# Memory keys as a fused layer's first products, its input loaded feature-major, and a gate's last chunks behind the attention heads

## The chip, the cores and the metric

One core of one Trainium2 chip runs the whole program. The metric is device time in microseconds (us) of one execution, the median of several. Beside it there is a profile of one execution by the hardware profiler.

The engines go by short names here: PE (TensorE) multiplies matrices; PEld is its load of weights; DVE (VectorE) and ACT (ScalarE) do elementwise work; POOL (GpSimd) does small work and starts accumulating DMAs; SP (SyncE) starts the loads. Each engine executes its own list of instructions strictly in the order in which the program wrote them, and waits on semaphores for the others.

## The reference

256 positions, width 1024, one layer, float32.

```python
n = rmsnorm(x) * g_mix
z = n @ w_in            # c_a, c_g, q, k, v, qi, ki, wi, gc, ga by columns
u = c_a * sigmoid(c_g)                      # the conv's input
u = causal_conv(u, 31 taps, per channel) + conv_b
y_conv = silu(layernorm(u)) @ w_conv_out
y_attn = attention(q, k, v, keys chosen by qi, ki, wi; 8 heads of 128) @ w_attn_out
h = x + (sigmoid(gc + b) * y_conv + sigmoid(ga + b) * y_attn) @ w_mix_out
m = rmsnorm(mem) * g_mem                    # 256 memory tokens
k2, v2 = split(m @ wx_kv)                   # 4 heads of 128
h = h + cross_attention(rmsnorm(h) * g_x @ wx_q, k2, v2) @ wx_o
h = h + relu(rmsnorm(h) * g_ffn @ w_ff1)**2 @ w_ff2
out = rmsnorm(h) * g_final
```

## The kernel before

**Products.** A float32 value is split into a high part of a shorter format (fp32r) and the low rest; a product is hi·hi + hi·lo + lo·hi. An activation's pair lies in a `Parts` tile (`n_p` for the normed input, `mem_p` for the memory, `o_p` for the heads' outputs, `u_p` for the normed conv), 8 blocks of 128 features (k, or kt) in two tiles of four. A tile of output is 128 features by 256 positions, and takes 8 k. In a *wide* tile the weights' high part is multiplied with both parts of the activation at once (512 columns), and the weights' low part with the high part (256 columns): two instructions for each k. The two 256-column halves of the bank are then added: ACT copies one half, DVE adds the other (`merge`).

**Weights.** `STREAM` lists the chunks of 1 MB (256 features each, two output tiles) in the order in which SP's queue loads them (`load`) and in which they are used. Names: conv (c_a and c_g), qi, ki, gc, ga, v, q, k, the memory's keys xk and values xv, ao (w_attn_out), co (w_conv_out), mix, and so on. A half chunk is split by ACT (`hi<-raw`) and DVE (`lo<-raw,hi`), a few halves ahead of its products. A chunk in `WHOLE` is not split: its products are made natively in float32, against an activation that is not split either. In the kernel before only the first conv chunk is such, against `n_f`.

**What sets the order.** Everything is written in the order in which the engines run it. Products of a stage are emitted tile by tile; between tiles `tick()` advances the chains in progress (generators: `head` for each attention head, `gate` for a gate, `memory` for the memory's norm, `layer_norm` for the conv) by one step, and then fills DVE's list with conv taps (`fill_one`) as long as the counted time of DVE is less than that of PE. So an edit of the chunk order moves steps of unlike chains against each other. Some taps go another way: ACT makes products and a POOL DMA accumulates them (`add_some`).

**The start.** `x` is loaded position-major (`x_rm`, two 512 KB loads), PE transposes it by 16 products (`pt_n`) after five warm-up products, ACT and DVE sum the squares of its rows (`ss_n`), POOL makes the reciprocal root (`rs_n`), PE spreads it over the partitions (`ps_rsb_n`), ACT and DVE apply the gain (`xg`), DVE multiplies (`n_f`) and the first conv products follow. The memory is read later in two layouts, `mem_rm` for the row norms and `mem_t` for the products, and nine steps of `memory` make its pair `mem_p`.

**The heads and behind them.** Each head is a chain: scores `ps_s`, masked maximum on DVE (`att_t`, `mx`), Exp on ACT (`att_p<-att_t,mx`), reciprocal on DVE, scale on ACT (`att_p<-att_p,sm`), transposes on PE (`ps_pt`), the product `ps_o`, the pair `o_p`. The last heads are covered by the products of xk and xv. Then ao (its merge gives `ya`, which is multiplied into the gate's tile `ga_t`) and co. Once all eight conv tiles have their 31 taps (`done`), `layer_norm` starts: PE averages over the features (`ps_mub`), DVE subtracts the mean (`acc<-acc,ps_mub`), ACT squares, DVE sums (`vs`), POOL makes the root, PE spreads it (`ps_rsb`), DVE multiplies, ACT applies Silu, and ACT and DVE write the pair `u_p`, two k at a time, which the co products read. An Exp, a Sigmoid and a Silu need different tables in ACT; changing them is an `ACT_TABLE_LOAD`.

Of the kernel before, what the change touches and what calls it, by code (L numbers as in the profile page):

```python
# [111 lines left out]
def block_kernel(ctx, tc, x, xt, mem, memt, wst, wki, vecs, convw, gout, out):  # L112
# [256 lines left out]
    nc.vector.tensor_copy(zero_r, zero)
# [10 lines left out]
    nc.scalar.activation(half, half, AF.Sigmoid, bias=0.0, scale=0.0)  # L380
    nc.gpsimd.memset(half, -0.5)
    ps = ps_aux("ps_warm")
    for j in range(5):
        nc.tensor.matmul(ps, zero_r[:, :P], zero_r, start=True, stop=True)
# [30 lines left out]
    ss = small.tile([P, 2], F32, tag="ss", name="ss_n")
    ptn = [ps_acc(f"pt_n{c}") for c in range(4)]
    xg = t8("xg")
    ss2 = small.tile([P, 2], F32, tag="ss2", name="ss2_n")
    nc.gpsimd.memset(ss2, EPS)
    junk = w2("junk_full", BF16, (P, D))  # L420
    act(junk, x_rm[:, 0, :], AF.Square, scale=1.0 / 32, accum_out=ss[:, 0:1])
# [4 lines left out]
    junk = w2("junk_half", BF16, (P, D))  # L426
    act(junk[:, : D // 2], x_rm[:, 1, : D // 2], AF.Square, scale=1.0 / 32, accum_out=ss[:, 1:2])
    dve.tensor_tensor_reduce(out=n_f[:, 0:2, :].rearrange("p k s -> p (k s)"), in0=x_rm[:, 1, D // 2 :],
                             in1=x_rm[:, 1, D // 2 :], scale=1.0 / D, scalar=EPS, op0=ALU.mult, op1=ALU.add,
                             accum_out=ss2[:, 1:2])  # L430
    dve.tensor_tensor(out=ss, in0=ss, in1=ss2, op=ALU.add)
    rs_n = power(ss, "n")
    rsb_n = spread(rs_n, "rsb_n")
    for kt in range(KT):
        src = ptn[kt // 2][:, (kt % 2) * S : (kt % 2) * S + S]
        if kt in (4, 6):
            dve.tensor_scalar(xg[:, kt, :], src, g_first[:, kt : kt + 1], None, ALU.mult)
        else:
            act(xg[:, kt, :], src, AF.Copy, scale=g_first[:, kt : kt + 1])
    for lo, hi in ((0, 1), (1, 2), (2, 4), (4, 6), (6, 8)):  # L440
        dve.tensor_tensor(out=n_f[:, lo:hi, :], in0=xg[:, lo:hi, :],
                          in1=rsb_n.unsqueeze(1).to_broadcast([P, hi - lo, S]), op=ALU.mult)
# [12 lines left out]
    def memory():
        mem_rm = t8("mem_rm", F32, (P, 2, D))
        mem_t = t8("mem_t")
# [12 lines left out]
        act(mrb, spread(rs_m, "mrb"), AF.Copy)  # L470
        for kt in range(KT + 1):
            if kt < KT:
                act(mem2.high(kt), mem_t[:, kt, :], AF.Copy, scale=g_mem[:, kt : kt + 1])
            if kt > 0:
                j = kt - 1
                dve.scalar_tensor_tensor(out=mem2.low(j), in0=mem_t[:, j, :], scalar=g_mem[:, j : j + 1],
                                         in1=mem2.high(j).bitcast(F32), op0=ALU.mult, op1=ALU.subtract)
            yield
# [51 lines left out]
    def conv_in(i):  # L530
# [106 lines left out]
        act(t, src, AF.Sigmoid, bias=b)
# [127 lines left out]
    kv = t8("kv", F32, (P, 2, XH * S))
    kx = kv[:, 0, :].rearrange("p (h n) -> p h n", h=XH)
    vx = kv[:, 1, :].rearrange("p (r n) -> p r n", r=2)
    for i in range(2):
        form_b("xk", i, mem2, copy_to(kx), ps_turn)
# [487 lines left out]
```

## Time and profile before

| | |
|---|---|
| time, median of 3 runs | 508.91 us (508.64 to 509.0) |
| the profiled execution's own time | 508.65 us |
| its span | 506.8 us |
| first conv product on PE | 8.74 us after the span's start |
| DMA read / written | 91.16 MB / 1.05 MB |

The span is the time from the first to the last recorded instruction; what the profiled execution took beyond it lies around it. In a chain row the first two numbers are start and length of a piece in us; in a timeline row start and summed length of a group of like instructions, with what ended the idle time ahead of it in square brackets. A group row has the count behind an x, then busy us and the mean of one in ns. Nearly all instructions of PE and DVE carry the line of the helper that records them (L77 before, L78 after), so they are told apart by their tiles.

### The profile page before, as it was taken

Reading aid. Unit: us, or ns where it says so; the run is one execution under the profiler, and the core shown is the slowest. Engines: PE = TensorE matmul, PEld = TensorE weight load, DVE = VectorE, ACT = ScalarE, POOL = GpSimd, SP = SyncE. Lnnn points to the kernel's source line nnn. Section 1 sums busy time; section 2 is a strip of 40 time slices with the busy share of each in tenths; the row PEclk is TensorE's granted clock in tenths of the full one; section 3 lists DMA queues with packets and bytes.
Section 4 is the critical chain, followed back from the end, with each engine's and each line's share of the span. In section 5 each row is a group of like instructions: output and inputs, shape, how many; then the busy total and the mean of one; then the engine's idle time right before and its main releaser. Section 6 shows DMA issues by size and latency. Waiting matters only on the chain.

```text
span 506.8 us, 7855 instructions
## 1 busy us (share of the span) xinstructions
PE 496.5 (98%) x2951; PEld 438.6 (87%) x2951; DVE 419.7 (83%) x806; ACT 314.6 (62%) x565; POOL 31.7 (6%) x49
## 2 busy tenths in 40 slices
PE   7999999999999999999999999999999999999994
PEld 5999998888888888888898999988888888888884
DVE  5999999999999799999899986699755666665565
ACT  7657777878666667678657666575444545544442
POOL 2002212221111100000000000000000000000000
PEclk9999999999999999999999999999999999999998
DMA  8959768899788634437644553445777744455302
GB/s 320 375 185 276 208 182 248 222 262 248 223 279 221 188 113 168 133 116 250 249 164 169 192 214 105 149 157 224 212 242 212 247 167 166 174 211 211 153 1 83
DMA packets 26502, 100.32 MB, mean 198 GB/s; under 512 B 10576, under 2 KB 11472, under 8 KB 15968
## 3 DMA queue, kind: packets, MB, share of 16 engines
q1 hardware_dynamic: 22400, 92.90, 52.5%
q0 software_dynamic: 3632, 6.59, 7.4%
q8 instruction: 23, 0.38, 0.3%
q10 hardware_dynamic: 432, 0.33, 0.2%
q14 instruction: 15, 0.12, 0.1%
HBM read 91.16 MB, written 1.05 MB: 182 GB/s over the span
## 4 chain that ended last, share of the span: by engine, by line
PE 95%; issue 1%; ACT 1%; DMA 1%; DVE 1%; POOLq 0%; POOL 0%; SPq 0%; DVEq 0%; ACTq 0%
PE ps_f L77 18%; PE ps_ff L77 16%; PE ps_conv L77 9%; PE ps_co L77 4%; PE ps_mix L77 4%; PE ps_ao L77 4%; PE ps_q L77 4%; PE ps_k L77 4%; PE ps_ga L77 4%; PE ps_gc L77 4%; PE ps_v L77 4%; PE ps_xo L77 3%; PE ps_qi L77 2%; PE ps_xk L77 2%; PE ps_xv L77 2%; PE ps_xq L77 2%
## 5 line engine op out<-in xcount | busy, mean ns | idle before, releaser
L77 DVE TENSOR_TENSOR lo<-raw,hi 128x1024 fp32r<-128x1024 f32 x163 | 196.8, 1216 | 5.0 <-ACT hi L189 3.4
L189 ACT ACTIVATE hi<-raw 128x1024 fp32r<-128x1024 f32 x163 | 168.8, 1048 | 1.6 <-DMA raw<-in_wst_dram 1.6
L77 PE MATMUL ps_f<-ff_p,hi 128*128 128x512 f32 x256 | 89.5, 396 | 0.0
L77 PE MATMUL ps_ff<-hi,fs 128*128 128x512 f32 (+1 forms) x256 | 80.4, 386 | 0.0
L77 DVE SCALAR_TENSOR_TENSOR acc<-u,cw,acc 128x234 f32<-128x234 f32 (+29 forms) x190 | 78.1, 462 | 0.3
L77 PE MATMUL ps_f<-ff_p,lo 128*128 128x256 f32 x256 | 66.1, 279 | 0.0
L77 PEld LDWEIGHTS ps_ff<-hi,fs 128*128 128x128 f32 x256 | 47.9, 188 | 9.2
L1084 ACT ACTIVATE ft<-ps_f 128x256 f32<-128x256 f32 x32 | 12.3, 383 | 70.0 <-PE ps_f L77 70.0
L77 PEld LDWEIGHTS ps_f<-ff_p,hi 128*128 128x128 f32 x256 | 46.7, 188 | 9.2
L77 DVE TENSOR_TENSOR ft<-ps_f,ft 128x256 f32<-128x256 f32 x32 | 13.5, 422 | 46.0 <-ACT ft L1084 46.0
L77 PEld LDWEIGHTS ps_f<-ff_p,lo 128*128 128x128 f32 x256 | 48.2, 188 | 2.7
L77 PE MATMUL ps_ff<-lo,fs 128*128 128x512 f32 (+1 forms) x128 | 49.4, 386 | 0.0
L77 PE MATMUL ps_conv<-n_p,hi 128*128 128x256 f32 x224 | 41.0, 285 | 0.0
L77 PEld LDWEIGHTS ps_conv<-n_p,hi 128*128 128x128 f32 x224 | 34.9, 192 | 0.8 <-issue 0.7
L77 PE MATMUL ps_conv<-n_p,lo 128*128 128x256 f32 x112 | 31.7, 283 | 0.0
L516 POOL DMA_DIRECT2D acc<-products x25 | 21.6, 866 | 125.3 <-ACT products L515 48.7
L77 PEld LDWEIGHTS ps_ff<-lo,fs 128*128 128x128 f32 x128 | 24.1, 188 | 4.9
L77 PE MATMUL ps_q<-n_p,hi 128*128 128x512 f32 x64 | 23.6, 406 | 0.0
L77 PE MATMUL ps_k<-n_p,hi 128*128 128x512 f32 x64 | 23.5, 407 | 0.0
L77 PE MATMUL ps_ao<-o_p,hi 128*128 128x512 f32 x64 | 22.6, 401 | 0.0
L77 PE MATMUL ps_co<-u_p,hi 128*128 128x512 f32 (+1 forms) x80 | 22.2, 351 | 0.0
L77 PE MATMUL ps_mix<-mix_p,hi 128*128 128x512 f32 (+1 forms) x80 | 22.2, 351 | 0.0
(246 smaller groups left out, 1009.4 us busy)
## 6 DMA issues: line engine op xcount, KB each, us to landing
raw<-in_wst_dram SPq DMA_DIRECT2D x80, 1024.0 KB, 4.9
acc<-products POOLq DMA_DIRECT2D x25, 256.0 KB, 5.0
raw<-in_wst_dram SPq DMA_DIRECT2D x4, 512.0 KB, 7.2
x_rm<-in_x_dram SPq DMA_DIRECT2D x2, 512.0 KB, 4.1
mem_rm<-in_mem_dram SPq DMA_DIRECT2D x1, 1024.0 KB, 8.7
mem_t<-in_memt_dram SPq DMA_DIRECT2D x1, 1024.0 KB, 10.7
h_t<-in_xt_dram SPq DMA_DIRECT2D x1, 1024.0 KB, 7.1
h_rm<-turned SPq DMA_DIRECT2D x16, 64.0 KB, 5.9
```

What stands on the lines that cost most here:

```text
L77: return fn(*args, **kwargs)
L189: act(hi, raw[:, ns], AF.Copy)
L516: nc.gpsimd.dma_start(acc[:, ts, :], prod, accum_op=ALU.add)
L1084: act(t, ps[:, S:], AF.Copy)
```

## The change

Two moves, and what goes with them.

*Memory keys first.* The two xk chunks are the stream's first. xk0 is multiplied natively (`native`) against `mem_g`, the gain times `mem_t`, and xk1 as two wide tiles against `mem_p`. `mem_t` and the first chunks are loaded in pieces that alternate on SP's queue. `x` comes feature-major as `x_t` from an input that the kernel already had, behind the first half of xk1, so the 16 transposes and the row sums go; ACT squares it, DVE adds over the k (`sums_n`), four small products (`ps_sq_n`) inside xk1's first tile sum over the partitions, and the root is spread inside xk1's second tile. `n_f` is made by four DVE steps with gain and root in one, and by four ACT scales with two DVE products. The warm-up is nine bf16 products instead of five. `vec` (the biases and gains) moves from POOL's queue to SP's, ahead of `cw`, and both behind the first conv chunks. The nine `mem_p` steps and the later `mem_t` load leave `memory`.

*The gate's last chunks.* Only ga 0 and 1 stand ahead of v; ga 2 and 3 stand behind q and k, where xk was. Their Sigmoid waits until all eight heads have had their Exp (`gate_late`), so that ACT's table changes once, and once more than before in all. `nused[0] < 5` becomes `< 7`, the number of half chunks used by then.

```diff
 STREAM = (
-    [("conv", i) for i in range(4)]
+    [("xk", i) for i in range(2)]
+    + [("conv", i) for i in range(4)]
...
-    + [("ga", i) for i in range(4)]
+    + [("ga", i) for i in range(2)]
     + [("v", i) for i in range(4)]
     + [(n, i) for i in range(4) for n in ("q", "k")]
-    + [("xk", i) for i in range(2)]
+    + [("ga", i) for i in range(2, 4)]
...
-WHOLE = (("conv", 0),)
+WHOLE = (("xk", 0), ("conv", 0))
...
-    x_rm = t8("x_rm", F32, (P, 2, D))
-    for rb in range(2):
-        nc.sync.dma_start(x_rm[:, rb, :], x[rb * P : (rb + 1) * P, :])
+    mem_t = t8("mem_t")
+    x_t = t8("x_t")
...
-    nc.gpsimd.dma_start(vec, vecs)
...
-    for parts in (2, 2, 1):
-        load(parts)
+    fetch(mem_t, memt, 0, 2)()
+    load((512, 1024), (fetch(mem_t, memt, 2, 5), fetch(mem_t, memt, 5, 8)))
+    load((1024,), (lambda: [fetch(x_t, xt, c, c + 4)() for c in (0, 4)],))
+    load((1024,))
+    load()
+    nc.sync.dma_start(vec, vecs)
     nc.sync.dma_start(cw, convw.rearrange("p (k t) -> p k t", k=KT))
-    load()
...
-    for j in range(5):
-        nc.tensor.matmul(ps, zero_r[:, :P], zero_r, start=True, stop=True)
+    for j in range(9):
+        nc.tensor.matmul(ps, zero[:, :P], zero, start=True, stop=True)
...
+    for kt in range(KT):
+        g = g_first[:, 1, kt : kt + 1]
+        if kt in (0, 2, 5):
+            act(mem_g[:, kt, :], mem_t[:, kt, :], AF.Copy, scale=g)
+        else:
+            dve.tensor_scalar(mem_g[:, kt, :], mem_t[:, kt, :], g, None, ALU.mult)
+    low_jobs_m = [mem_parts(kt) for kt in range(0, KT, 2)]
+    for job in low_jobs_m:
+        job()
+    ps_k0 = native(("xk", 0), 0, mem_g)
+    split_high()
+    split_low()
+    act(kx[:, 0, :], ps_k0, AF.Copy)
+    ps_k1 = native(("xk", 0), 1, mem_g)
+    adds = [x_square(kt) for kt in range(0, KT, 2)]
+    act(kx[:, 1, :], ps_k1, AF.Copy)
+    for add in adds:
+        add()
+    split_high()
+    load()
+    ws, banks = [], []
+    ws.append(weights("xk", 1, 0, KT))
+    banks.append(ps_acc("ps_xk10"))
+    tile_b(banks[0], ws[0], mem2, range(6), True)
+    ps = ps_aux("ps_sq_n")
     for rb in range(2):
-        for kt in range(KT):
-            pe.transpose(ptn[kt // 2][:, (kt % 2) * S + rb * P : (kt % 2) * S + rb * P + P],
-                         x_rm[:, rb, kt * P : kt * P + P], ident)
...
+        for j in range(2):
+            pe.matmul(ps[:, 2 * rb : 2 * rb + 2], sums_n[:, j, rb * P : rb * P + P], onesd[:, :2], start=j == 0,
+                      stop=j == 1)
+    ms = small.tile([P, 2], F32, tag="ms", name="ms_n")
+    dve.tensor_scalar(ms, ps[:, :4].rearrange("p (r t) -> p r t", r=2)[:, :, 0], EPS, None, ALU.add)
+    rs_n = power(ms, "n")
+    split_low()
+    tile_b(banks[0], ws[0], mem2, range(6, KT), True)
+    ws.append(weights("xk", 1, 1, KT))
+    banks.append(ps_acc("ps_xk11"))
+    ps = banks[1]
+    for lo, hi in ((0, 3), (3, 6)):
+        for kt in range(lo, hi):
+            pe.matmul(ps, ws[1][0][:, kt, :], mem2.both(kt), start=kt == 0, stop=False)
+        for kt in range(lo, hi):
+            pe.matmul(ps[:, S:], ws[1][1][:, kt, :], mem2.high(kt), start=False, stop=False)
+        if lo == 0:
+            rsb_n = spread(rs_n, "rsb_n")
+    tile_b(ps, ws[1], mem2, range(6, KT), True)
+    for kt in range(4, KT):
+        act(n_f[:, kt, :], x_t[:, kt, :], AF.Copy, scale=g_first[:, 0, kt : kt + 1])
+    for kt in range(4):
+        dve.scalar_tensor_tensor(out=n_f[:, kt, :], in0=x_t[:, kt, :], scalar=g_first[:, 0, kt : kt + 1], in1=rsb_n,
+                                 op0=ALU.mult, op1=ALU.mult)
+    for kt in (4, 6):
+        dve.tensor_tensor(out=n_f[:, kt : kt + 2, :], in0=n_f[:, kt : kt + 2, :],
+                          in1=rsb_n.unsqueeze(1).to_broadcast([P, 2, S]), op=ALU.mult)
...
     def memory():
...
-        nc.sync.dma_start(mem_t, memt)
...
-        for kt in range(KT + 1):
-            if kt < KT:
-                act(mem2.high(kt), mem_t[:, kt, :], AF.Copy, scale=g_mem[:, kt : kt + 1])
...
@@ in head
+        exped.append(h)
...
+    def gate_late(ct, ps):
+        yield from merge(ga_t[:, ct, :], ps)
+        while len(exped) < NH:
+            yield
+        act(ga_t[:, ct, :], ga_t[:, ct, :], AF.Sigmoid, bias=bga[:, ct : ct + 1])
+
+    late = []
+    for i in range(2, 4):
+        form_b("ga", i, n2, lambda ct, ps: late.append(start(gate_late(ct, ps))), ps_turn)
...
-    for c in heads:
+    for c in heads + late:
         finish(c)
```

Three places show how the lists of instructions differ. The first is PE at the start. The numbers behind the names only keep tiles apart. Before:

```order
L384 MATMUL ps_warm<-zero_r 128x512 x5
L77 MATMUL pt_n_128<-ident,x_rm 128x128 x2
...
L77 MATMUL pt_n_131<-ident,x_rm 128x128 x2
L77 MATMUL ps_rsb_n<-ident,rs_n 128x128 x2
L77 MATMUL ps_conv_203<-n_f,raw_89 128x256 x8
L77 MATMUL ps_conv_218<-n_f,raw_89 128x256 x8
L77 MATMUL ps_conv_237<-n_p_124,hi_0_183 128x256 x2
```

After (`ps_xk_156` and `_170` are the native tiles of xk0, `_195` and `_224` those of xk1, `ps_conv_282` the first conv tile):

```order
L390 MATMUL ps_warm<-zero 128x512
L78 MATMUL ps_xk_156<-mem_g,raw_88 128x256 x8
L78 MATMUL ps_xk_170<-mem_g,raw_88 128x256 x8
L78 MATMUL ps_xk_195<-mem_p_133,hi_0_165 128x512
...
L78 MATMUL ps_xk_195<-mem_p_134,hi_0_165 128x512
L78 MATMUL ps_sq_n<-onesd,sums_n 128x2 x4
L78 MATMUL ps_xk_195<-mem_p_134,lo_0_166 128x256
...
L78 MATMUL ps_xk_224<-mem_p_133,hi_1_190 128x512 x3
L78 MATMUL ps_xk_224<-mem_p_133,lo_1_191 128x256 x3
L78 MATMUL ps_rsb_n<-ident,rs_n 128x128 x2
L78 MATMUL ps_xk_224<-mem_p_133,hi_1_190 128x512
...
L78 MATMUL ps_conv_282<-n_f,raw_99 128x256 x8
```

The four xk tiles, with the sums of x and the spread inside them, now stand ahead of the first conv products, and the 16 transposes are gone.

The second is ACT at the last heads, from the last head's Exp (the rows with `sm` on the left) to the scale of the head before it. Before:

```order
L273 ACTIVATE o_p_1715<-ps_o_2459 128x256
L728 ACTIVATE att_p_2466,sm_2428<-att_t_2382,mx_2427 128x128
L728 ACTIVATE att_p_2466,sm_2428<-att_t_2382,mx_2427 128x256
L333 ACTIVATE kv<-ps_xk_2442 128x256
L189 ACTIVATE hi_0_2479<-raw_2309 128x1024
L734 ACTIVATE att_p_2424<-att_p_2424,sm_2375 128x128
L734 ACTIVATE att_p_2424<-att_p_2424,sm_2375 128x256
L189 ACTIVATE hi_1_2502<-raw_2309 128x1024
```

After:

```order
L276 ACTIVATE o_p_1669<-ps_o_2417 128x256
L778 ACTIVATE att_p_2424,sm_2386<-att_t_2340,mx_2385 128x128
L778 ACTIVATE att_p_2424,sm_2386<-att_t_2340,mx_2385 128x256
L820 ACT_TABLE_LOAD
L820 ACTIVATE ga_t<-ga_t,vec 128x256 x3
L336 ACTIVATE ga_t<-ps_ga_2400 128x256
L192 ACTIVATE hi_0_2442<-raw_2268 128x1024
L785 ACTIVATE att_p_2382<-att_p_2382,sm_2333 128x128
L785 ACTIVATE att_p_2382<-att_p_2382,sm_2333 128x256
L820 ACTIVATE ga_t<-ga_t,vec 128x256
```

A table load and three sigmoids now stand between the last Exp and the copy of the last tile's merge, the next split and the scale of head 6; a fourth sigmoid follows.

The third is PE behind the last head (`ps_o` is its product, `ps_ao` the first tile of ao). Before:

```order
L77 MATMUL ps_xv_2475<-hi_1_2439,mem_p_191 128x512
L77 MATMUL ps_o_2584<-ptr_2560,v_rm 128x128 x3
L77 MATMUL ps_mub<-usum,onesd 128x256
L77 MATMUL ps_ao_2614<-o_p_1714,hi_0_2479 128x512
L77 MATMUL ps_ao_2614<-o_p_1714,lo_0_2480 128x256 x2
L77 MATMUL ps_ao_2614<-o_p_1714,hi_0_2479 128x512
```

After:

```order
L78 MATMUL ps_o_2549<-ptr_2522,v_rm 128x128 x3
L78 MATMUL ps_ao_2563<-o_p_1668,hi_0_2442 128x512
L78 MATMUL ps_ao_2563<-o_p_1668,lo_0_2443 128x256 x2
...
L78 MATMUL ps_ao_2563<-o_p_1669,lo_0_2443 128x256
L78 MATMUL ps_ao_2563<-o_p_1669,hi_0_2442 128x512
L78 MATMUL ps_mub<-usum,onesd 128x256
L78 MATMUL ps_ao_2604<-o_p_1668,hi_1_2465 128x512
```

The product of the conv's mean stood ahead of the first ao tile and now stands behind it.

On DVE, from the pair of the last head (`o_p<-ps_o`) to the sums of squares, before:

```order
L77 TENSOR_TENSOR lo_0_2536<-raw_2390,hi_0_2535 128x1024
L77 TENSOR_TENSOR o_p_1715<-ps_o_2584,o_p_1715 128x256
L77 TENSOR_TENSOR acc<-acc,ps_mub 128x512 x3
L77 TENSOR_TENSOR vs<-vs,sq_vr_2598 128x512
L77 TENSOR_TENSOR acc<-acc,ps_mub 128x512
```

After:

```order
L78 TENSOR_TENSOR lo_0_2498<-raw_2348,hi_0_2497 128x1024
L78 TENSOR_TENSOR o_p_1669<-ps_o_2549,o_p_1669 128x256
L78 SCALAR_TENSOR_TENSOR acc<-u,cw,acc 128x226
L78 TENSOR_TENSOR usum<-usum,acc 128x256
L78 TENSOR_TENSOR lo_1_2533<-raw_2348,hi_1_2532 128x1024
L78 TENSOR_TENSOR acc<-acc,ps_mub 128x512 x3
L78 TENSOR_TENSOR vs<-vs,sq_vr_2588 128x512
L78 TENSOR_TENSOR acc<-acc,ps_mub 128x512
```

One conv tap, its sum and a split now stand between the pair of the last head and the subtraction of the mean.

More of the change, by code (lines that the diff above doesn't have):

```diff
@@ L159, in block_kernel, with load @@
     high_jobs, low_jobs = [], []
-    def load(parts=1):
+    def load(cuts=(), between=()):
         if nload[0] >= len(STREAM):
@@ L169, in load @@
         src = wki if key[0] == "ki" else wst[INDEX[key]]
-        for q in range(parts):
-            ns = slice(q * n // parts, (q + 1) * n // parts)
-            nc.sync.dma_start(raw[:, ns], src[:, ns])
+        between = list(between)
+        for lo, hi in zip((0, *cuts), (*cuts, n)):
+            nc.sync.dma_start(raw[:, lo:hi], src[:, lo:hi])
+            if between:
+                between.pop(0)()
         if key in WHOLE:
@@ L249, in tick @@
                 chains.remove(c)
-        while (len(fill) > 1 or (fill and (len(done) > 5 or nused[0] < 5))) and dve.total < pe.total - 1000:
+        while (len(fill) > 1 or (fill and (len(done) > 5 or nused[0] < 7))) and dve.total < pe.total - 1000:
             fill_one()
@@ L350, in copy_to, with fetch @@
         return lambda ct, ps: copy_out(dst[:, ct, :], ps)
-    g_first = cst.tile([P, KT], F32, name="g_first")
-    nc.scalar.dma_start(g_first, vecs[:, 5 * KT : 6 * KT])
-    x_rm = t8("x_rm", F32, (P, 2, D))
-    for rb in range(2):
-        nc.sync.dma_start(x_rm[:, rb, :], x[rb * P : (rb + 1) * P, :])
+    g_first = cst.tile([P, 2, KT], F32, name="g_first")
+    nc.scalar.dma_start(g_first, vecs[:, 5 * KT : 7 * KT].rearrange("p (j k) -> p j k", j=2))
+    mem_t = t8("mem_t")
+    x_t = t8("x_t")
     vec = cst.tile([P, 72], F32, name="vec")
-    nc.gpsimd.dma_start(vec, vecs)
-    bgc, bga, cvb, lng, lnb, g_mix, g_mem, g_x, g_ffn = (vec[:, 8 * j : 8 * j + 8] for j in range(9))
+    bgc, bga, cvb, lng, lnb, _, _, g_x, g_ffn = (vec[:, 8 * j : 8 * j + 8] for j in range(9))
     cw = cst.tile([P, KT, TAPS], F32, name="cw")
-    for parts in (2, 2, 1):
-        load(parts)
+    def fetch(dst, src, lo, hi):
+        return lambda: nc.sync.dma_start(dst[:, lo:hi, :], src[:, lo:hi, :])
+    fetch(mem_t, memt, 0, 2)()
[4 more added lines that the diff above has]
+    nc.sync.dma_start(vec, vecs)
     nc.sync.dma_start(cw, convw.rearrange("p (k t) -> p k t", k=KT))
-    load()
-    zero = w2("zero")
+    zero = cst.tile([P, 512], BF16, name="zero")
     nc.vector.memset(zero, 0.0)
-    zero_r = cst.tile([P, 512], F32R, name="zero_r")
-    nc.vector.tensor_copy(zero_r, zero)
     ident = cst.tile([P, P], F32, name="ident")
@@ L410, in spread @@
         return ps[:, :S]
+    mem_g = t8("mem_g")
+    mem2 = parts_t8("mem_p")
+    kx = cst.tile([P, XH, S], F32, name="kx")
     n2 = parts_t8("n_p")
     n_f = t8("n_f")
[L415 to L421, printed above, removed]
@@ L422, in block_kernel @@
-    for rb in range(2):
-        for kt in range(KT):
-            pe.transpose(ptn[kt // 2][:, (kt % 2) * S + rb * P : (kt % 2) * S + rb * P + P],
-                         x_rm[:, rb, kt * P : kt * P + P], ident)
[L426 to L442, printed above, removed]
+    sums_n = w2("sums_n", F32, (P, 2, S))
@@ new lines, in native, with mem_parts, low @@
+    def native(key, half, src, kts=range(KT), ps=None):
+        ps = ps or ps_mm(f"ps_{key[0]}{key[1]}{half}")[:, :S]
+        for kt in kts:
+            pe.matmul(ps, whole[key][:, half * KT + kt, :], src[:, kt, :], start=kt == 0, stop=kt == KT - 1)
+        return ps
+    def mem_parts(kt):
+        act(mem2.high(kt, 2), mem_g[:, kt : kt + 2, :], AF.Copy)
+        def low():
+            dve.tensor_tensor(out=mem2.low(kt, 2), in0=mem_g[:, kt : kt + 2, :], in1=mem2.high(kt, 2).bitcast(F32),
+                              op=ALU.subtract)
+        return low
@@ new lines, in x_square @@
+    def x_square(kt):
+        src = x_t[:, kt : kt + 2, :]
+        if kt == 0:
+            act(sums_n, src, AF.Square)
+            return lambda: None
+        sq = w2(f"sq_n{kt}", F32, (P, 2, S))
+        act(sq, src, AF.Square)
+        return lambda: dve.tensor_tensor(out=sums_n, in0=sums_n, in1=sq, op=ALU.add)
+    for kt in range(KT):
[4 more added lines that the diff above has]
+            dve.tensor_scalar(mem_g[:, kt, :], mem_t[:, kt, :], g, None, ALU.mult)
@@ L443, in block_kernel @@
+    for kt in range(4):
[4 more added lines that the diff above has]
+                          in1=rsb_n.unsqueeze(1).to_broadcast([P, 2, S]), op=ALU.mult)
     for c in range(0, KT, 2):
         split(n2.high(c, 2), n2.low(c, 2), n_f[:, c : c + 2, :])
+    for ct in range(2):
+        merge_now(kx[:, 2 + ct, :], banks[ct])
@@ L448, in block_kernel @@
     pe.total = dve.total = 0.0
-    mem2 = parts_t8("mem_p")
     rs_m = cst.tile([P, 2], F32, name="rs_m")
@@ L470, in memory @@
         act(mrb, spread(rs_m, "mrb"), AF.Copy)
-        for kt in range(KT + 1):
-            if kt < KT:
-                act(mem2.high(kt), mem_t[:, kt, :], AF.Copy, scale=g_mem[:, kt : kt + 1])
[L474 to L478, printed above, removed]
     u = t8("u")
@@ L525, in conv_tile @@
         else:
-            for kt in range(KT):
-                pe.matmul(ps[:, :S], whole[key][:, half * KT + kt, :], n_f[:, kt, :], start=kt == 0, stop=kt == KT - 1)
+            native(key, half, n_f, ps=ps[:, :S])
         return ps
@@ L637, in gate @@
         act(t, src, AF.Sigmoid, bias=b)
-    for kind, dst, b in (("gc", gc_t, bgc), ("ga", ga_t, bga)):
-        for i in range(4):
+    for kind, dst, b, n in (("gc", gc_t, bgc, 4), ("ga", ga_t, bga, 2)):
+        for i in range(n):
             form_b(kind, i, n2, lambda ct, ps: start(gate(dst[:, ct, :], ps, b[:, ct : ct + 1])), ps_turn)
@@ L748, in head @@
         headed.append(h)
-    heads, headed = [], []
+    heads, headed, exped = [], [], []
     def qk(name):
@@ L763, in block_kernel @@
         form_b("k", i, n2, after_k, ps_turn)
[L765 to L769, printed above, removed]
+    def gate_late(ct, ps):
[6 more added lines that the diff above has]
+        form_b("ga", i, n2, lambda ct, ps: late.append(start(gate_late(ct, ps))), ps_turn)
+    vx = t8("vx", F32, (P, 2, XH * HD))
     form_a("xv", 0, mem2, vx, (rs_m[:, 0:1], rs_m[:, 1:2]))
-    for c in heads:
+    for c in heads + late:
         finish(c)
```

1 line of the change is left out of this document (removed).

## The prediction

> **What bounds the kernel now.** I read the page's shares first, then the chain that ended last, then TensorE's own waits, then the two stages that are touched.
>
> ```profile
> span 506.8 us, 7855 instructions
> PE 496.5 (98%) x2951; PEld 438.6 (87%) x2951; DVE 419.7 (83%) x806; ACT 314.6 (62%) x565; POOL 31.7 (6%) x49
> PE 95%; issue 1%; ACT 1%; DMA 1%; DVE 1%; POOLq 0%; POOL 0%; SPq 0%; DVEq 0%; ACTq 0%
> PE ps_warm L384 <- DVE zero_r L369: 1.9, 1, 1.9
> PE ps_rsb_n L77 <- POOL rs_n L389: 0.9, 1, 0.9
> PE ps_conv L77 <- DVE n_f L77: 0.6, 1, 0.6
> 10.00:250.00 240.00, 240.00 (x1510) 215.25 (x1509) 230.02 (x492) 172.86 (x326) 27.02 (x31) 1.00 0.70 219
> ```
>
> TensorE carries 95% of the chain. The three rows after that are all its waits (total, times, longest), all before 8.74 us. The last row is one stretch of 240 us by engine: PE, its weight loads, DVE, ACT, POOL, granted clock, DMA share, GB/s. PE is busy in all of it, and DVE in 230.02. So the change can gain only at the start, where PE is fed by nothing yet; and any wait that it makes PE take later is lost in full. The profiled execution took 508.65 us around its 506.8 us span; the median of the runs is 508.91, 0.26 more. I add that at the end.
>
> **The change: what it takes out of the middle.** Four xk tiles leave the stage of the last heads. In the chain they are
>
> ```profile
> 194.05 2.79 PE ps_xk L77 x16
> ...
> 197.49 2.78 PE ps_xk L77 x16
> ...
> 201.26 2.78 PE ps_xk L77 x16
> ...
> 205.04 2.82 PE ps_xk L77 x16
> ```
>
> which sums to 11.17 us. The four ga tiles are as many products as before, two of them now in this place, so they cost nothing by themselves. What decides is by how much the first conv product starts later than 8.74: less than 11.17 is a gain.
>
> **The start.**
>
> ```profile
> 1.18 4.50 DMA x_rm<-in_x_dram
> 8.74 24.52 PE ps_conv L77 x176
> 5.71 0.63 ACT L427 ACTIVATE junk_half<-x_rm 128x512 bf16<-128x512 f32 x1 [0.17 <-DMA x_rm<-in_x_dram]
> 14.06 1.06 ACT L189 ACTIVATE hi<-raw 128x1024 fp32r<-128x1024 f32 x1 [0.69 <-DMA raw<-in_wst_dram]
> L77 PE MATMUL ps_conv<-n_f,raw x32: 379/379/483, 8.7 to 15.6; 128*128 128x256 f32 x32
> 1.92 2.50 PE L384 MATMUL ps_warm<-zero_r 128*128 128x512 f32 x5 [1.92 <-DVE zero_r L369]
> 6.75 0.88 DVE L77 TENSOR_SCALAR xg<-pt_n,g_first 128x256 f32<-128x256 f32 x2
> 9.05 2.42 ACT L273 ACTIVATE n_p<-n_f 128x512 fp32r<-128x512 f32 x4 [0.43 <-DVE n_f L77]
> L189 ACT ACTIVATE hi<-raw 128x1024 fp32r<-128x1024 f32 x163 | 168.8, 1048 | 1.6 <-DMA raw<-in_wst_dram 1.6
> L77 DVE TENSOR_TENSOR lo<-raw,hi 128x1024 fp32r<-128x1024 f32 x163 | 196.8, 1216 | 5.0 <-ACT hi L189 3.4
> 6.95 0.72 POOL L389 TENSOR_TENSOR rs_n<-ss_n,half 128x2 f32<-128x2 f32 x1 [3.86 <-DVE ss_n L77]
> ```
>
> Bytes: 1 MiB (both x_rm) had landed at 5.7, 4 MiB at 14.06, so a MiB takes (14.06 − 5.7)/3 = 2.79 us. In the new order the last of mem_t stands at 1.5 MiB: 7.1; xk0 at 2.0: 8.5; the first half of xk1 at 2.5: 9.9; x_t at 3.0 and 3.5: 11.3 and 12.7; the rest of xk1 at 4.0: 14.06.
>
> Prices: a native tile (n_f row: 32 instructions from 8.7 to 15.6 are two tiles) is 6.83/2 = 3.41, 0.43 for each k; a split tile 2.79, 0.35 for each k. The whole chunk xk0 thus costs 2 × (3.41 − 2.79) = 1.25 more than it did.
>
> TensorE's sequence. The nine warm-up products end near 5.4 (the five in the row are some 0.45 apart; the memset is shorter than memset and cast). The products for k 0 to 4 take 2.15: 7.55. The gain of k 6 and 7 is two DVE steps of 0.44 behind 7.1, so k 7 starts near 8.4 after hand-offs, and the first tile ends at 8.85. Second native tile: 12.26. xk1's first tile, six k: 2.09, 14.35 (its hi is done at 10.95, its lo at 12.15 at the latest, by the prices above). Now PE asks for the sums of squares: two squares of x_t after 12.7 (0.6 each, n_p row), adds of about 0.6 on DVE, done at 14.5; four small products 0.66, as the four ps_s in a later fence; 15.2. Last two k: 0.70, 15.9. Second tile: three hi 0.69, 16.6; its lo (landed 14.06, hi to 15.1, lo behind the mean on DVE to 16.55) lets three lo follow, 0.36, 16.95. The power takes 0.72 on POOL from 15.4 and is ready at 16.2, so the spread does not wait: 0.22, 17.2. Rest 1.05 + 0.70: 18.9. Hand-offs 0.2: **conv starts at 19.1**, 10.36 later than 8.74. Gain 11.17 − 10.36 = **0.8**.
>
> Bounds: PE alone needs 2 × 3.41 + 2 × 2.79 + 0.68 + 0.22 = 13.3; dense from 5.0 it would start conv at 18.3 (gain 1.6). With a microsecond of late sums or lo, 20.0 (loss 0.1). The wh products, squares, gains and the four scaled n_f on ACT are beside PE: n_f's first k is one DVE step behind the spread, 17.7, before PE is free. The two loads put on SP's queue (vec, cw) are first read in the first conv's taps; they stand behind conv0 and conv1, 0.16 MB, 0.4 us of stream, and conv2's chunk at 7.2 MiB lands near 23, eight microseconds before its products. The mem_t load in the middle goes and x is read twice; both lie under a DMA share of 0.70.
>
> A rule speaks against the cut first loads. The Trainium skill (DMA: Bandwidth & Descriptors, § Measured) says to batch DMAs to 1 MiB or more for 75% of peak. By that rule the pieces of 256 to 512 KB would land later; this trace ran at 418 GB/s from 8 to 10 us with halves of 512 KB in flight, so I leave the stream's rate as it is in the sum.
>
> ```profile
> DMA packets 236, 0.84 MB, mean 418 GB/s; under 512 B 32, under 2 KB 32, under 8 KB 236
> DMA packets 39, 0.15 MB, mean 217 GB/s; under 512 B 2, under 2 KB 2, under 8 KB 39
> ```
>
> The second of these rows is 6.2 to 6.9 us: a dip, which stays as the rival below.
>
> **The last heads, ACT.**
>
> ```profile
> 210.94 0.79 ACT L734 ACTIVATE att_p<-att_p,sm 128x128 f32<-128x128 f32 x2
> L637 ACT ACTIVATE ga_t<-ga_t,vec 128x256 f32<-128x256 f32 x8 | 4.0, 496 | 0.0
> 230.70 1.05 ACT L189 ACTIVATE hi<-raw 128x1024 fp32r<-128x1024 f32 x1
> 231.77 1.28 ACT L691 ACT_TABLE_LOAD   x1
> 233.06 0.20 ACT L691 ACTIVATE table<-table 128x1 f32<-128x1 f32 x1
> 196.84 0.66 PE ps_s L77 x4
> 214.03 0.33 PE ps_pt L77 x3
> ```
>
> Between the last head's Exp and the scale of head 6, which PE's transposes take at 214.03, now stand a table load and three sigmoids: 1.28 + 3 × 0.4 to 0.5 = 2.5 to 2.8. The scale ends at 211.63 before, so 214.1 to 214.4: PE waits **0.25** (0 to 0.7). The load is 1.28 with an ACTIVATE directly ahead and another directly behind.
>
> The Trainium skill (ScalarE: Activation LUTs, § What ACT_TABLE_LOAD costs) gives 1283 ns for the load and 1380 ns of drain. The rows agree with the load and show no drain. By the page this term would be 1.6 and the sum 1.4 higher.
>
> **The last heads, DVE, and the normed conv.**
>
> ```profile
> 221.51 0.43 PE ps_mub L77 x2
> 221.94 8.38 PE ps_ao L77 x48
> 222.30 1.87 DVE L77 TENSOR_TENSOR acc<-acc,ps_mub 128x512 f32<-128x512 f32 x3
> 229.42 0.42 DVE L77 TENSOR_TENSOR ya<-ps_ao,ya 128x256 f32<-128x256 f32 x1
> 229.87 0.42 DVE L77 TENSOR_TENSOR ga_t<-ya,ga_t 128x256 f32<-128x256 f32 x1
> 233.85 0.69 DVE L77 TENSOR_TENSOR acc<-acc,ps_rsb 128x512 f32<-128x512 f32 x1 [0.42 <-PE ps_rsb L77]
> 244.49 0.63 ACT L698 ACTIVATE u_p<-acc 128x512 fp32r<-128x512 f32 x1
> 245.77 0.68 DVE L77 TENSOR_TENSOR u_p<-acc,u_p 128x512 fp32r<-128x512 f32 x1
> 247.05 0.62 PE L77 MATMUL ps_co<-u_p,hi 128*128 128x512 f32 x2
> ```
>
> The deferred sigmoids also hold up ACT's copy of the last ga tile, so DVE takes its merge late, with 14 taps still behind it (11 behind the last xk merge before), and the products of the mean (ps_mub) now stand behind the first ao tile in PE's order instead of ahead of it. So DVE may start acc − mean at 222.30 + 2.79 = 225.1 at best. From there to the last u_p DVE took 245.77 − 222.30 = 23.47. Now it has one lo fewer (−1.14), one ya and ga_t pair more (+0.80), the wait of 0.42 goes, and the last u_p must wait some 0.4 for its silu on ACT, which had 0.65 to spare (244.49 + 0.63 against 245.77). Sum 23.1: it starts at 248.2 and ends at 248.85. PE wants it at 247.05 + 0.25 = 247.3: it waits **1.55** (0.7 to 2.2; the reorder could also turn out covered, 0, if DVE reaches the mean earlier than I follow). What is late next: nothing, since the co products read their last chunk's lo with microseconds to spare and DVE then catches up.
>
> **Sum**: −0.8 + 0.25 + 1.55 = +1.0. 508.65 + 1.0 = 509.65, on the median's scale **509.9**.
>
> **The rivals.**
> (a) The waits at the heads vanish: DVE has 10 us idle in 240, and 9 steps of mem_p and two lo fewer than before, so it could come ahead; with a start at 18.5 the gain is 1.4 and nothing is paid: 507.5. Against it: the mean stands in PE's order behind the ao tile, however early DVE is. It needs the wait at ps_co under 0.3.
> (b) The start slips. If the dip of 217 GB/s lasts, or sums and lo of xk1 come a microsecond late, conv starts at 20.3, the gain of 0.8 is a loss of 0.4, and with the 1.8 of waits the time is 508.91 + 2.2 = 511.1. Against it: the bytes asked for by 14.06 are as many as before. The point from which this decides is a start later than 19.9, where the first half alone loses. This ends on the other side of (a) and of no change.
> (c) The drain of the page is real when the switch comes between Exp and Sigmoid: 509.9 + 1.4 = 511.3. No row of the trace bears it out.
> (d) The start gains as forecast and half of the waits come: +0.1, 509.0; the change then does nothing that can be told.
>
> **Chances.** 0.2% of 508.91 is 1.0 us, about what a measurement can tell from no change. My forecast 0.45 (which lies on the bound, so half of it counts as within, half as slower), (a) 0.15, (b) 0.16, (c) 0.05, (d) 0.19. Faster 0.15; within 0.22 + 0.19 = 0.41; slower 0.23 + 0.16 + 0.05 = 0.44. The range leaves out most of (a) and the end of (c): 508.1 to 511.2. The likeliest case alone is 509.2 to 510.6.
>
> **What would show it.** The first ps_conv product near 19.1; no PE wait between 10 us and the heads; a wait of ps_pt on ACT's scale of some 0.25 and one of ps_co on DVE's u_p of some 1.5. Conv near 18.4 and no wait at ps_co makes (a); conv after 19.9 (b); ACT idle over a microsecond after the new table load (c). The forecast is wrong if PE's wait at ps_co is under 0.5, or if PE waits for ACT in heads that I did not name.

## The result, and the profile after

| | before | changed |
|---|---|---|
| median | 508.92 us, 6 runs (508.58 to 509.0) | 512.17 us, 6 runs (511.76 to 514.16) |
| ratio | | 1.0076, interval 1.0056 to 1.0096 |
| profiled execution, span | 508.65, 506.8 | 514.08, 512.3 |

The change made the kernel 3.25 us slower. I had forecast 509.9 and a range to 511.2: the sign held, the size did not. The six runs are 511.76, 511.9, 512.1, 512.24 and then 514.08 and 514.16; the profiled one is of the upper two, which decides how its rows are read.

The chain's shares by engine, and all of PE's waits (us in total, times, longest):

```profile
PE 80%; DVE 11%; ACT 4%; issue 2%; DMA 1%; SPq 0%; POOLq 0%; POOL 0%; DVEq 0%; ACTq 0%
PE ps_xk L78 <- ACT mem_g L453: 2.1, 2, 1.7
PE ps_warm L390 <- DVE zero L375: 1.2, 1, 1.2
PE ps_xk L78 <- DMA raw<-in_wst_dram: 0.8, 2, 0.4
PE ps_co L78 <- DVE u_p L78: 0.6, 2, 0.3
PE ps_co L78 <- ACT u_p L748: 0.3, 1, 0.3
```

DVE now has 11% of the chain (1% before), and PE waits in two places: for the gain of `mem_t` at the start, and for `u_p` at co. Two points on PE's list give the account. The first conv product, and the last pair of co's first tile, stood at 8.74 and 247.05 before; the last ps_ff product, ahead of the final norm, gives the third:

```profile
498.31 0.28 PE L77 MATMUL ps_ff<-hi,fs 128*128 128x256 f32 x1
```

```profile
24.06 3.18 PE L78 MATMUL ps_conv<-n_f,raw 128*128 128x256 f32 x14
253.09 0.73 PE L78 MATMUL ps_co<-u_p,hi 128*128 128x512 f32 x2 [0.34 <-DVE u_p L78]
504.49 0.28 PE L78 MATMUL ps_ff<-hi,fs 128*128 128x256 f32 x1
```

The start lost 24.06 − 8.74 − 11.17 = 4.15. From the conv to the last ps_ff another 6.18 − 4.15 = 2.03. Behind it the program took 0.68 less (7.81 for 8.49), a tail that lasted between 7.8 and 8.6 in the profiles of this study, though none of the kernels edits it; the cause is not known.

**The start.** PE by groups, with what ended each wait, and ACT's gain of the last third of `mem_t`:

```profile
5.15 1.10 PE L78 MATMUL ps_xk<-mem_g,raw 128*128 128x256 f32 x4 [0.42 <-DMA raw<-in_wst_dram]
6.61 1.13 PE L78 MATMUL ps_xk<-mem_g,raw 128*128 128x256 f32 x4 [0.36 <-ACT mem_g L453]
8.12 0.67 PE L78 MATMUL ps_xk<-mem_g,raw 128*128 128x256 f32 x2 [0.38 <-DMA raw<-in_wst_dram]
10.49 6.70 PE L78 MATMUL ps_xk<-mem_g,raw 128*128 128x256 f32 x22 [1.71 <-ACT mem_g L453]
19.12 0.95 PE L78 MATMUL ps_sq_n<-onesd,sums_n 128*128 128x2 f32 x8
9.93 0.51 ACT L453 ACTIVATE mem_g<-mem_t,g_first 128x256 f32<-128x256 f32 x1 [3.38 <-DMA mem_t<-in_memt_dram]
```

The last piece of `mem_t` landed at 9.9, where the forecast had 7.1. A native product is two instructions of PE, and the counts of rows are of instructions. The 22 from 10.49 (k 5 to 7 of the first tile and the whole second tile) took until 16.85, 0.29 each in place of 0.21. Three stretches of 3.41 us, cut where the granted clock changes, tell why (length, then PE, PEld, DVE, ACT, POOL busy, granted clock, DMA share, GB/s):

```profile
4.09:7.50 3.41, 2.63 (x11) 1.45 (x9) 0.97 (x3) 1.02 (x2) 0.00 (x0) 1.00 0.96 286
7.50:10.91 3.41, 1.32 (x6) 0.69 (x5) 0.62 (x2) 0.98 (x3) 0.00 (x0) 1.00 1.01 395
10.92:14.33 3.41, 3.41 (x10) 2.70 (x9) 3.25 (x5) 3.41 (x8) 0.00 (x0) 0.50 1.02 418
```

PE was busy for 1.32 of the middle one, and in the next its clock was granted at half.

**The heads.**

```profile
213.79 1.28 ACT L820 ACT_TABLE_LOAD   x1
215.09 1.31 ACT L820 ACTIVATE ga_t<-ga_t,vec 128x256 f32<-128x256 f32 x3
217.52 0.79 ACT L785 ACTIVATE att_p<-att_p,sm 128x128 f32<-128x128 f32 x2
217.96 0.83 PE L78 MATMUL ps_pt<-ident,att_p 128*128 128x128 f32 x3
218.55 0.48 PE L78 MATMUL ps_xv<-hi,mem_p 128*128 128x512 f32 x1
227.72 0.42 DVE L78 TENSOR_TENSOR usum<-usum,acc 128x256 f32<-128x256 f32 x1
228.06 1.22 DVE L78 TENSOR_TENSOR lo<-raw,hi 128x1024 fp32r<-128x1024 f32 x1
228.59 0.59 PE L78 MATMUL ps_mub<-usum,onesd 128*128 128x256 f32 x2
229.22 1.88 DVE L78 TENSOR_TENSOR acc<-acc,ps_mub 128x512 f32<-128x512 f32 x3
251.18 0.50 PE L78 MATMUL ps_co<-u_p,hi 128*128 128x512 f32 x1 [0.24 <-DVE u_p L78]
252.37 0.38 PE L78 MATMUL ps_co<-u_p,lo 128*128 128x256 f32 x1 [0.33 <-ACT u_p L748]
252.35 0.69 DVE L78 TENSOR_TENSOR u_p<-acc,u_p 128x512 fp32r<-128x512 f32 x1 [0.43 <-ACT u_p L748]
```

The first co product moved by 4.41 (244.84 to 249.25), 0.26 more than the start's 4.15. That 0.26 is a net figure. At ps_pt PE lost 0.48: from the product ahead of the three transposes to the one behind them it took 0.96 (217.59 to 218.55), where it took 0.48 before (213.63 to 214.11). The first conv tile gave back 0.18: before, PE came to it from a wait, and two of its first instructions took 0.32 and 0.28 to the next one, where here they take 0.21 and 0.22. The last pair moved by 6.04: 1.63 more, around three waits. The page counts 0.9 us of them as idle; the 1.63 is taken from starts, since the recorded lengths of neighbouring products overlap. The load of the table is 1.28 and the sigmoids follow at once.

The last sum of the mean (`usum`) ended at 228.14, 0.45 ahead of ps_mub. Had ps_mub stood ahead of the first ao tile (225.72), PE would have waited there for DVE. So its place in PE's order cost the norm 0.45 at most; the rest is DVE's.

### The profile page after: what moved, and what is told of

It reads as the page before. It is cut to its first block, busy times and chain, and to the rows that moved or that the text cites. A ratio compares the mean times of both kernels' runs of the same rounds, so it can differ in the third digit from the quotient of the medians.

```text
span 512.3 us, 7837 instructions
## 1 busy us (share of the span) xinstructions
PE 501.0 (98%) x2947; PEld 439.2 (86%) x2947; DVE 417.9 (82%) x802; ACT 314.3 (61%) x561; POOL 31.7 (6%) x47
## 4 chain that ended last, share of the span: by engine, by line
PE 80%; DVE 11%; ACT 4%; issue 2%; DMA 1%; SPq 0%; POOLq 0%; POOL 0%; DVEq 0%; ACTq 0%
PE ps_f L78 17%; PE ps_ff L78 16%; PE ps_conv L78 9%; PE ps_q L78 4%; PE ps_k L78 4%; PE ps_gc L78 4%; PE ps_ga L78 4%; PE ps_v L78 4%; DVE lo L78 4%; PE ps_xo L78 3%; PE ps_xk L78 2%; PE ps_qi L78 2%; PE ps_xq L78 2%; DMA mem_t<-in_memt_dram 1%; DVE gc_t L78 1%
## 5 line engine op out<-in xcount | busy, mean ns | idle before, releaser
L78 DVE TENSOR_TENSOR lo<-raw,hi 128x1024 fp32r<-128x1024 f32 (+1 forms) x161 | 194.5, 1217 | 3.9 <-ACT hi L192 2.3
L192 ACT ACTIVATE hi<-raw 128x1024 fp32r<-128x1024 f32 (+1 forms) x161 | 166.7, 1048 | 2.9 <-DMA raw<-in_wst_dram 2.5
L78 DVE SCALAR_TENSOR_TENSOR acc<-u,cw,acc 128x234 f32<-128x234 f32 (+25 forms) x190 | 78.2, 461 | 0.3
L78 PE MATMUL ps_ga<-n_p,hi 128*128 128x512 f32 x64 | 23.1, 404 | 0.0
```

The costliest lines, as they stand in the source:

```text
L78: return fn(*args, **kwargs)
L192: act(hi, raw[:, ns], AF.Copy)
```

## The experiments

All were timed beside the kernel before on the same chip (medians 508.70 to 508.77).

**1. The deferred gate alone.** The kernel before with ga 2, 3 and xk exchanged, cut to the lines that matter:

```diff
-    + [("ga", i) for i in range(4)]
+    + [("ga", i) for i in range(2)]
+    + [("xk", i) for i in range(2)]
...
-    + [("xk", i) for i in range(2)]
+    + [("ga", i) for i in range(2, 4)]
```

Here too ga 2 and 3 go through `gate_late`.

> The kernel before, with its own start; only ga 2, 3 and xk 0, 1 exchange places (xk ahead of v, ga 2, 3 with the deferred sigmoids at the last heads). Theory A, the heads' terms as forecast: the table load and three sigmoids hold ps_pt by 0.25 us; the wait at ps_co is not from ACT but from DVE, which in the changed kernel has 11.2 us less of PE's time and only some 9 us less work ahead of the mean, and here has as much of both as before. So +0.3 us, 509.2 (0 to 0.8), ps_mub ahead of the first ao product, no wait at ps_co over 0.3. Rival B, the deferred gate itself costs the whole 1.9 us that the changed kernel loses between its first conv product and the second co tile: 510.8.

Measured 509.28 (ratio 1.0014, 1.0004 to 1.0023), +0.51. Its mean and the last pair of co's first tile:

```profile
222.00 0.60 PE L78 MATMUL ps_mub<-usum,onesd 128*128 128x256 f32 x2
247.70 0.62 PE L78 MATMUL ps_co<-u_p,hi 128*128 128x512 f32 x2
```

No wait at co. Between the products around ps_pt PE took 0.96 here too (213.80 to 214.76, 0.48 before). So the table and the sigmoids cost that half microsecond, and the 1.63 at co are not theirs.

**2. DVE relieved.**

```diff
-        while (...) and dve.total < pe.total - 1000:
+        while (...) and dve.total < pe.total:
...
+        left_out = range(1, 7) if i == 1 else ()
-        queue = [tap(i, s) for s in range(1, TAPS) if s not in delays.get(i // 2, ())]
+        queue = [tap(i, s) for s in range(1, TAPS) if s not in delays.get(i // 2, ()) and s not in left_out]
```

> The changed kernel with six of the 31 conv taps of one channel block left out (2.4 us of DVE's work), and taps filled until DVE's counted time reaches PE's in place of 1000 ns less. The mean's product then stands ahead of the first ao product, as in the kernel before. Theory A, the wait at ps_co is DVE's deficit (11.2 us of PE's time taken out ahead of the heads, only some 9 us of DVE's): with DVE relieved the three waits at ps_co, 1.6 us in sum, fall under 0.4, and the time to 510.6 (510.3 to 511.0). Rival B, the wait comes from ACT's deferred gate, which is as it was: 512.2, waits as before.

Measured 510.72 (1.0043, 1.0028 to 1.0058). PE's waits, all of them:

```profile
PE ps_xk L78 <- ACT mem_g L453: 1.7, 1, 1.7
PE ps_warm L390 <- DVE zero L375: 1.2, 1, 1.2
PE ps_xk L78 <- DMA raw<-in_wst_dram: 0.2, 1, 0.2
```

None at co, in a kernel that leaves six taps of one block out. The control with the filling rule alone, and all taps in it:

> The changed kernel with the same edit of the filling rule alone, all taps in it: the control of the run with six taps left out. Theory A: ps_mub stays behind the first ao tile, the waits at ps_co stay near 1.6, the time near 512.2. Rival C, the filling rule and not DVE's load is what matters: 510.6, as with six taps left out.

Measured 513.46 (1.0113, 1.0063 to 1.0163), four runs from 512.55 to 518.53, with the waits of 0.6 and 0.3 at co as in the changed kernel. Theory A: the chain of the conv's norm is late because DVE is. The balance fits: from the first conv product to acc − mean, PE's list lost 11.17 us of products, and DVE's busy time fell by only 8.2 (204.41 to 196.20).

**3. The other way to relieve DVE**, more taps by ACT and POOL: `[(3, 5000)] * 8` becomes `[(3, 3000)] * 12`.

> The changed kernel with four more pairs of conv taps on the way over ACT and POOL (twelve entries with a pause of 3000 in place of eight with 5000), so DVE has eight taps or 3.2 us less to do ahead of the layer norm, and the mean's product stands ahead of the first ao tile again. Theory A, DVE's deficit sets the wait at ps_co: that wait falls from 1.6 to under 0.4 and the time by 1.2 to 1.6, to 510.7. Rival B, the wait follows the mean's place behind ps_ao or ACT, which has more to do here: no gain or a loss, 512 or more.

Measured 520.4 (1.0202, 1.0161 to 1.0242). A miss, for a reason that neither theory had; DVE's longest wait of its own:

```profile
DVE acc L78 <- DMA acc<-products: 9.9, 1, 9.9
```

An accumulating DMA of 256 KB took 5.8 us from issue to landing here (the median of 29; 6.1 in the changed kernel), and POOL waited for the one before in 13 places. Asked for every 3 us they were late, the taps queued behind them, and heads behind the taps: PE waited 7.1 us for DVE ahead of ps_xv and ps_s, and its clock was at half for 6.8 us behind the longest of these waits (3.9). It says nothing on DVE's deficit.

**4. Larger first pieces.**

```diff
-    fetch(mem_t, memt, 0, 2)()
-    load((512, 1024), (fetch(mem_t, memt, 2, 5), fetch(mem_t, memt, 5, 8)))
+    fetch(mem_t, memt, 0, 4)()
+    load((1024,), (fetch(mem_t, memt, 4, 8),))
```

> The changed kernel, mem_t and xk0's raw chunk loaded in alternating pieces of 512 KB with rows of 4 KB, where it has pieces of 256 and 384 KB with rows of 2 and 3 KB. Theory A, small pieces let the 16 DMA engines run out of step, so that mem_t's last piece landed at 9.9 us when 2.4 MB had moved: with 512 KB the last piece of mem_t lands near 7.2, PE waits for nothing after 7.5, its clock holds, the first conv product is near 20 in place of 24.1, the time 510 to 510.5. Rival B, the piece size does not matter and what is late is the stream's beginning: conv stays beyond 22, the time 511.5 to 512.5.

Measured 511.53 (1.0053, 1.0038 to 1.0068), four runs within 0.11, none of 514.

```profile
6.12 1.97 PE L78 MATMUL ps_xk<-mem_g,raw 128*128 128x256 f32 x8 [0.94 <-DMA raw<-in_wst_dram]
8.58 5.45 PE L78 MATMUL ps_xk<-mem_g,raw 128*128 128x256 f32 x24 [0.49 <-DVE mem_g L78]
20.90 6.42 PE L78 MATMUL ps_conv<-n_f,raw 128*128 128x256 f32 x29
```

Less than I expected: mem_t was whole at 8.2, not 7.2, and the time fell by 0.6 where I had forecast 1.7 to 2.2. Neither theory holds as it was put. What the DMA engines had moved by the moment at which 1.5 MiB (1.57 MB) were whole: in the changed kernel (9.9 us), in this one (8.2), and in the kernel before (7.65), a row each:

```profile
DMA packets 1083, 2.41 MB, mean 243 GB/s; under 512 B 241, under 2 KB 241, under 8 KB 1083
```

```profile
DMA packets 689, 2.02 MB, mean 246 GB/s; under 512 B 198, under 2 KB 198, under 8 KB 689
```

```profile
DMA packets 677, 1.90 MB, mean 248 GB/s; under 512 B 208, under 2 KB 208, under 8 KB 677
```

The mean rate is the same; what differs is how much of later pieces had already come when the piece that PE waits for was whole: 0.84, 0.45 and 0.33 MB.

**5. PE kept busy while it waits**, by nine products on zeros ahead of k 2, 4 and 5 of the first tile.

> The changed kernel with nine small products on zeros put between the native products of the first tile (one ahead of k 2, one ahead of k 4, seven ahead of k 5), where PE waits for the loads. Theory A, the half clock that the profile grants from 10.9 to 14.3 us follows PE's idling from 8.8 to 10.5: with PE kept busy the granted clock is 1.00 after the warm-up, the 22 native products that took 6.4 us take 4.7, and runs of 514 do not occur: 511.9, all within 0.5. Rival B, the drop comes whatever PE does: a run of 514 among the six and a clock of 0.994 stay.

Measured 512.62 (1.0074, 1.0059 to 1.0089), four runs from 512.27 to 512.94. The clock from 11 to 14.3 us, and the native products of xk0 and conv0:

```profile
11.00:14.30 3.30, 3.30 (x17) 2.91 (x16) 3.12 (x5) 3.30 (x7) 0.00 (x0) 1.00 1.04 423
10.59 5.02 PE L78 MATMUL ps_xk<-mem_g,raw 128*128 128x256 f32 x22
22.50 4.69 PE L78 MATMUL ps_conv<-n_f,raw 128*128 128x256 f32 x21
```

The 22 instructions end at 15.26 in place of 16.85, and no run is of 514. The median is 0.7 over what I expected and no better than the four lower runs of the changed kernel. Those have no profile, but a mean granted clock is on record for every run: 0.996 to 0.998 for these four, 0.994 for the two at 514 (a stretch of 3.41 us at half clock takes 0.003 off the mean). So the four most likely had no half clock, and a filler nothing to mend in them.

**6. Two queues, and mem_t whole.** Both from experiment 4: `mem_t`'s two pieces on ACT's queue; or `mem_t` as one load of 1 MiB ahead of the weights.

> The changed kernel with its first loads in pieces of 512 KB, mem_t's two on ACT's queue and the weights on SP's. Theory A, mem_t's last piece is late because it stands behind and beside other pieces on one queue and the stream itself takes 2.8 us for a MiB with a dip from 6 to 7: on two queues both streams share the engines, all of the first 1.5 MiB land near 8, as on one (8.2): conv near 21, 511.5. Rival B, SP's queue is the limit (an issue each 0.45 us): mem_t lands by 6.5, raw by 7, conv near 19.5, the time 510.

> The changed kernel with mem_t as a single load of 1 MiB ahead of xk0's first 512 KB. Theory A, the larger the pieces the nearer they land to the stream's rate: mem_t near 6, raw near 8.2, PE then waits for nothing; but it starts at 8.2 and has 13.9 us to do, conv near 22, 512.5, with the clock dropped in some runs since PE idles from 5.2 to 8.2. Rival B, rows of 8 KB make the stream faster: raw by 7.2, conv by 21, 511.5.

Measured 515.57 (1.0157, 1.0101 to 1.0214) and 514.22 (1.0115, 1.0098 to 1.0131). PE's longest wait in each, and the two stretches of 3.41 us behind the warm-up of the second:

```profile
PE ps_xk L78 <- ACT mem_g L454: 3.9, 1, 3.9
```

```profile
PE ps_xk L78 <- DMA raw<-in_wst_dram: 3.3, 1, 3.3
4.09:7.50 3.41, 0.63 (x3) 0.10 (x1) 1.40 (x5) 1.63 (x4) 0.00 (x0) 1.00 0.90 333
7.50:10.91 3.41, 2.92 (x7) 2.41 (x8) 2.50 (x4) 2.22 (x5) 0.00 (x0) 0.50 1.02 402
```

With two queues the first piece of mem_t landed only at 8.5 and the second at 11.0, while PE waited for nothing of the weights. So a second queue did not help, and rival B's limit on SP's queue is out. Both kernels idle PE for over 3 us, and both profiles show the half clock behind it.

**7. What the findings recover.** Experiment 4, and: the sums of squares folded on DVE (two small products for four); five of seven additions to `usum` on POOL. Of the edit, the line for `usum`:

```diff
+                    add = dve.tensor_tensor if len(done) > 6 else nc.gpsimd.tensor_tensor
```

> The changed kernel with three mends: first loads in pieces of 512 KB; the two halves of x's sums of squares added on DVE, so that PE has two small products in place of four; five of the seven additions to usum on POOL in place of DVE (1.7 us of DVE's work), by which the mean's product stands ahead of the first ao product again. Theory A (late loads and DVE's deficit are all that the forecast missed or paid): conv from 20.5, 0.6 behind the kernel before after the 11.17 us of key tiles; 0.26 at ps_pt; nothing or up to 0.4 at ps_co: 509.8 (509.4 to 510.2). Rival B, the additions on POOL hold up its accumulating DMAs or the mean, and the wait returns in another place: 511 or more.

Measured 509.62 (1.0025, 1.0014 to 1.0037). PE's waits beside the warm-up's, and the two points:

```profile
PE ps_xk L78 <- DMA raw<-in_wst_dram: 1.3, 1, 1.3
PE ps_xk L78 <- DVE mem_g L78: 0.5, 1, 0.5
20.66 6.64 PE L78 MATMUL ps_conv<-n_f,raw 128*128 128x256 f32 x30
248.10 0.62 PE L78 MATMUL ps_co<-u_p,hi 128*128 128x512 f32 x2
```

1.7 us less on DVE were enough, without any change of the filling rule. A last try to reach the kernel before, raw's first half cut in two pieces of 256 KB and the sigmoids behind the last head's scale:

> The kernel relieved with two more mends: the four deferred sigmoids behind the last head's scale instead of ahead of head 6's; and the first loads in the order mem_t k 0 to 3, raw k 0 to 3 (256 KB), mem_t k 4 to 7, raw k 4 to 7. Theory A: ps_pt waits no more (0.26 less); raw's first piece lands at 5.2 and the last that the first tile needs still near 8.1, but as raw and not as mem_t with the gain behind it, so the first tile ends 0.4 earlier: 509.0 (508.7 to 509.3), level with the kernel before. Rival B, the pieces of 256 KB spread the engines again and land later (9 us or more), and ACT's 3 us of table and sigmoids hold up the copy for o_p of head 6 and with it DVE: 509.6 or more.

Measured 510.89 (1.0042, 1.0028 to 1.0056): rival B in both parts, though ps_pt did not wait any more, as theory A had it.

```profile
PE ps_xk L78 <- DMA raw<-in_wst_dram: 2.2, 2, 1.1
PE ps_mub L78 <- DVE usum L78: 0.5, 1, 0.5
221.43 0.42 DVE L78 TENSOR_TENSOR o_p<-ps_o,o_p 128x256 fp32r<-128x256 f32 x1 [1.49 <-ACT o_p L276]
```

The cut pieces landed a microsecond later, and the sigmoids held up ACT's copy for `o_p` and so the mean. No version here beats the kernel before.

## Why the prediction was right and wrong

Per profile, the first conv product, what the start lost after the 11.17 us of key tiles, and what was lost from there to the last ps_ff product:

| | conv | start | rest |
|---|---|---|---|
| forecast | 19.1 | −0.8 | 1.8 |
| changed | 24.06 | 4.15 | 2.03 |
| filler | 22.50 | 2.59 | 2.03 |
| pieces of 512 KB | 20.90 | 0.99 | 2.03 |
| six taps out | 22.28 | 2.37 | 0.45 |
| relieved | 20.66 | 0.75 | 0.36 |
| deferred gate alone | 8.92 | 0.18 | 0.54 |

**The heads were right in their sum, with some luck.** 1.8 forecast, 2.03 measured. ps_pt: 0.25 forecast, 0.48 measured, within the stated 0 to 0.7; that the net is 0.26 is due to 0.18 from the first conv tile, which the sum does not have. The wait at co: 1.55 forecast, 1.63 measured, with the last u_p waiting 0.43 for ACT (0.4 forecast). The cause was half right. I put DVE's late merge, and with it the deferred gate, at its head, and made the place of the mean behind the first ao tile the bound; with the gate alone the wait does not come, DVE's own sum was ready only 0.45 ahead of the mean's product in that place, and with DVE relieved the wait goes. Rival (c), the drain of the Trainium skill (ScalarE: Activation LUTs, § What ACT_TABLE_LOAD costs), is out: the sigmoids start 0.02 behind the load, and PE's loss at ps_pt is 0.48, not the 1.6 of that rival.

**The start was wrong by 4.96**, in three terms of the sum. *The landings:* the step "in the new order the last of mem_t stands at 1.5 MiB: 7.1" reads a position in the queue as a time. It was 9.9, so the first tile ended at 11.77 by full clock for 8.85: 2.92. The step drew a straight line from 5.7 to 14.06 through the dip that I quoted, and took each piece to be whole when as many bytes had moved. Of the 2.8 us, 0.55 is the line (1.5 MiB were whole at 7.65 in the kernel before), another 0.55 stays with pieces of 512 KB (8.2), and 1.7 came with the smaller pieces. The prediction named late landings of small pieces and left them out of its sum, on a rate of 418 GB/s; the mean rate was indeed as before, and the pieces were late all the same. *The clock:* 22 instructions at 0.29 for 0.21, 1.68 in this profile; the sum put it at nothing and no rival named it. *The rest,* 0.37: four small products are eight instructions, 0.81 for 0.66; the other 0.22 was not traced further. Rival (b) had the right mechanism with a bound that was too near: "the bytes asked for by 14.06 are as many as before" was no argument, since the pieces, not the bytes, were late.

**The sum.** −0.8 + 2.92 + 0.37 = 2.5 is what the filler and the six taps show for the start at full clock (2.59, 2.37). With 2.03 and a tail shorter by up to 0.7 this makes 3.8 to 4.5, where the four lower runs are at 2.8 to 3.3; the landings of those unprofiled runs are not known, so 0.5 to 1.3 us of the median stay open.

The granted clock: the Trainium skill (TensorE: Matmul & The Clock Gate, Part 1) gives free-running windows of 3413 ns and half rate after an idle one. The rows agree on the length, and show that the window need not be idle: PE was busy for 1.32 of it here and 0.63 with mem_t loaded whole.

Not tried: whether mem_t's layout in memory, and not the pieces alone, makes its landing later than x's was.

## What to carry to other kernels

A piece's place in a queue did not give the time at which it landed; price a start that is fed by small pieces by rows of such pieces, and add what later pieces take from it. Where a tile is moved out of a stage that fills both PE and DVE, count what leaves each of them: 11.17 us of PE's products left this stage and only 8.2 us of DVE's work, and PE lost 1.63 waiting for DVE's chain. And keep PE busy while the first data come, or price a window at half clock.
